# Taking most of the last maximum while the last rows still load, and splitting the early stores

## The chip, the cores and the metric

The kernel runs on one core of a Trainium2 chip. The metric is device time in microseconds (us) of one execution.

In the profile, DVE is VectorE, ACT is ScalarE, POOL is GpSimd and SP is SyncE, which in the kernels before and after issues the loads. A name with a q (SPq, POOLq) is that engine's sequencer. L48 is line 48 of the kernel. The *span* is what the profile covers, from the first instruction to the last; it is 1.8 to 1.9 us shorter than the time. Each run lists the span of every execution, rounded to 0.1 us. The trace of each profiled execution has the span to 0.001 us (320.545 before); stretches that run to the end of the span are taken from it.

## The reference

```python
B, N, D = 8, 4096, 512
gram = np.matmul(x, y.transpose(0, 2, 1))
diag = np.diagonal(gram, axis1=1, axis2=2)
diag = diag - diag.max(axis=-1, keepdims=True)
exp = np.exp(diag)
return exp / exp.sum(axis=-1, keepdims=True)
```

Only the diagonal is needed: 4096 dot products of length 512 in each of 8 batches, then a softmax over the 4096 numbers of a batch. The work on the data takes less time than reading it: 134 MB have to be read.

## The kernel before

A batch lies on 128 partitions with R = 32 rows each, so its dot products are a tile of 128 x 32: "column r" holds the dot products of row r of every partition. The first five batches share one softmax (group a), the next two share another (group b), and the last batch has its own. Only this last one cannot hide behind loads. To keep it short, the last batch is loaded in ever smaller pieces, down to one row.

```python
def dot_row(b, r):                      # one column of 128 dot products
    nc.vector.scalar_tensor_tensor(out=xt[:, r, :], in0=xt[:, r, :], scalar=1.0,
        in1=ys[:, r, :], op0=Alu.mult, op1=Alu.mult, accum_out=diag[:, b, r : r + 1])

def group_out(name, b0, n, ssum):       # scale and store a group
    # ... (reciprocal and scaling cut)
    nc.scalar.dma_start(out=ov[:, b0 : b0 + n, :], in_=res[:, b0 : b0 + n, :])

def last_softmax(b):
    db, rb = diag[:, b, :], res[:, b, :]
    # ... (columns cut)
    nc.vector.tensor_reduce(out=mxp, in_=db, axis=X, op=Alu.max)
    nc.gpsimd.partition_all_reduce(out_ap=mx, in_ap=mxp, channels=P, reduce_op=bass_isa.ReduceOp.max)
    nc.vector.tensor_single_scalar(out=nmx, in_=mx, scalar=-1.0, op=Alu.mult)
    nc.scalar.activation(out=rb, in_=db, func=Act.Exp, bias=nmx, scale=1.0, accum_out=sump)
    nc.gpsimd.partition_all_reduce(out_ap=ssum, in_ap=sump, channels=P, reduce_op=bass_isa.ReduceOp.add)
    nc.vector.reciprocal(out=rc, in_=ssum)
    nc.vector.tensor_single_scalar(out=rb, in_=rb, scalar=rc, op=Alu.mult)
    nc.scalar.dma_start(out=ov[:, b, :], in_=rb)

# ... (batches 0 to 6 cut)
b = B - 1
r0 = 0
for n in (8, 8, 8, 4, 2, 1, 1):
    load_x(b, r0, n)                    # both on the SyncE queue
    load_y(b, r0, n)
    for r in range(r0, r0 + n):
        if r == 2:
            second = group_exp("b", B - 3, 2)
        if r == 10:
            group_out("b", B - 3, 2, second)
        dot_row(b, r)
    r0 += n
last_softmax(b)
```

In this program every DMA signals its completion on one of eight semaphores, in turn (DMA 0 on the first, DMA 8 on the first again); the trace numbers them S99 to S101 and S103 to S107. In the traces, a DMA that is to use a semaphore is issued only when the DMA that used it before has landed. So adding one store shifts which earlier DMA each later load waits for.

Of the kernel before, what the change touches and what calls it, by code (L numbers as in the profile page):

```python
# [1 line left out]

# [5 lines left out]


@with_exitstack
def kernel(
    ctx: ExitStack,
    tc: tile.TileContext,
    x: bass.AP,
    y: bass.AP,
    out: bass.AP,
):
    nc = tc.nc
    ctx.enter_context(tc.manual_schedule())  # L20
    f32 = mybir.dt.float32
    Alu = mybir.AluOpType
    Act = mybir.ActivationFunctionType
    X = mybir.AxisListType.X
    B, N, D = x.shape
    P = nc.NUM_PARTITIONS
    R = N // P
    wide = B - 2


    xv = x.rearrange("b (p r) d -> b p r d", p=P)
    yv = y.rearrange("b (p r) d -> b p r d", p=P)
    ov = out.rearrange("b (p r) -> p b r", p=P)

    big = ctx.enter_context(tc.tile_pool(name="big", bufs=1))
    small = ctx.enter_context(tc.tile_pool(name="small", bufs=1))


    xs = [big.tile([P, R, D], f32, name=f"xs{i}") for i in range(2)]
    ys = big.tile([P, R, D], f32, name="ys")  # L40
    diag = small.tile([P, B, R], f32, name="diag")
    res = small.tile([P, B, R], f32, name="res")

    def column(name, n):
        return small.tile([P, n], f32, name=name)

    def load_x(b, r0, n):
        nc.sync.dma_start(out=xs[b % 2][:, r0 : r0 + n, :], in_=xv[b, :, r0 : r0 + n, :])  # L48

    def load_y(b, r0, n):  # L50
        nc.sync.dma_start(out=ys[:, r0 : r0 + n, :], in_=yv[b, :, r0 : r0 + n, :])

    def dots_wide(b, r0, n):
        xt = xs[b % 2][:, r0 : r0 + n, :]
        nc.vector.tensor_tensor(out=xt, in0=xt, in1=ys[:, r0 : r0 + n, :], op=Alu.mult)  # L55

    def sums_wide(b):
        nc.vector.tensor_reduce(out=diag[:, b, :], in_=xs[b % 2], axis=X, op=Alu.add)  # L58

    def dot_row(b, r):  # L60
        xt = xs[b % 2]
        nc.vector.scalar_tensor_tensor(  # L62
            out=xt[:, r, :],
            in0=xt[:, r, :],
            scalar=1.0,
            in1=ys[:, r, :],
            op0=Alu.mult,
            op1=Alu.mult,
            accum_out=diag[:, b, r : r + 1],
        )  # L70

    def group_exp(name, b0, n):

        mxp, mx, nmx, sump, ssum = (column(name + s, n) for s in ("mxp", "mx", "nmx", "sump", "ssum"))
        nc.vector.tensor_reduce(out=mxp, in_=diag[:, b0 : b0 + n, :], axis=X, op=Alu.max)  # L75
        nc.gpsimd.partition_all_reduce(out_ap=mx, in_ap=mxp, channels=P, reduce_op=bass_isa.ReduceOp.max)  # L76
        nc.scalar.mul(nmx, mx, -1.0)  # L77
        for i in range(n):
            nc.scalar.activation(  # L79
                out=res[:, b0 + i, :], in_=diag[:, b0 + i, :], func=Act.Exp,  # L80
                bias=nmx[:, i : i + 1], scale=1.0, accum_out=sump[:, i : i + 1],
            )
        nc.gpsimd.partition_all_reduce(out_ap=ssum, in_ap=sump, channels=P, reduce_op=bass_isa.ReduceOp.add)  # L83
        return ssum

    def group_out(name, b0, n, ssum):
        rc = column(name + "rc", n)
        nc.vector.reciprocal(out=rc, in_=ssum)  # L88
        for i in range(n):
            rb = res[:, b0 + i, :]  # L90
            nc.scalar.activation(out=rb, in_=rb, func=Act.Copy, scale=rc[:, i : i + 1])  # L91
        nc.scalar.dma_start(out=ov[:, b0 : b0 + n, :], in_=res[:, b0 : b0 + n, :])

    def last_softmax(b):
        db, rb = diag[:, b, :], res[:, b, :]
        mxp, mx, nmx, sump, ssum, rc = (column("l" + s, 1) for s in ("mxp", "mx", "nmx", "sump", "ssum", "rc"))
        nc.vector.tensor_reduce(out=mxp, in_=db, axis=X, op=Alu.max)  # L97
        nc.gpsimd.partition_all_reduce(out_ap=mx, in_ap=mxp, channels=P, reduce_op=bass_isa.ReduceOp.max)  # L98
        nc.vector.tensor_single_scalar(out=nmx, in_=mx, scalar=-1.0, op=Alu.mult)  # L99
        nc.scalar.activation(out=rb, in_=db, func=Act.Exp, bias=nmx, scale=1.0, accum_out=sump)  # L100
        nc.gpsimd.partition_all_reduce(out_ap=ssum, in_ap=sump, channels=P, reduce_op=bass_isa.ReduceOp.add)  # L101
        nc.vector.reciprocal(out=rc, in_=ssum)  # L102
        nc.vector.tensor_single_scalar(out=rb, in_=rb, scalar=rc, op=Alu.mult)  # L103
        nc.scalar.dma_start(out=ov[:, b, :], in_=rb)

    for b in range(wide):
        load_x(b, 0, R)
        for r0 in (0, R // 2):
            load_y(b, r0, R // 2)
            dots_wide(b, r0, R // 2)  # L110
        if b == wide - 1:
            group_out("a", 0, wide - 1, first)
        sums_wide(b)
        if b == wide - 2:
            first = group_exp("a", 0, wide - 1)

    b = B - 2
    load_x(b, 0, R)
    for r0 in (0, R // 2):
        load_y(b, r0, R // 2)  # L120
        for r in range(r0, r0 + R // 2):
# [5 lines that stand above are left out]
        load_x(b, r0, n)  # L127
        load_y(b, r0, n)
        for r in range(r0, r0 + n):
            if r == 2:  # L130
                second = group_exp("b", B - 3, 2)
            if r == 10:
                group_out("b", B - 3, 2, second)
            dot_row(b, r)
        r0 += n
    last_softmax(b)


# [1 line left out]
_INS = ['x', 'y']  # L140
_OUTS = [((8, 4096), 'float32')]


# [23 lines left out]
```

## Time and profile before

| | before |
|---|---|
| time, median of the first runs | 322.76 us (322.57 to 322.77) |
| span of the profiled execution | 320.5 us |
| last row of y landed | 314.97 us |
| start of the last row's product to end of span | 5.48 us |
| last store issued to end of span | 2.41 us |

First, lines of the page of the kernel before: the span, the busy time of VectorE, the two DMA queues (packets, MB, share of 16 engines' span; q1 carries the loads and q10 the stores), and the lines of the chain of work that ended last.

```profile
span 320.5 us, 318 instructions
...
DVE 248.9 (78%) x154; ACT 6.2 (2%) x26; POOL 3.3 (1%) x10
...
q1 hardware_dynamic: 5040, 134.22, 97.4%
q10 hardware_dynamic: 1072, 0.13, 0.3%
...
DMA ys<-in_y_dram 74%; DVE xs L55 16%; DVE xs L62 4%; DMA out_dram<-res 3%; SPq L48 0%; POOLq L162 0%; ACT res L91 0%; POOL lmx L98 0%; DVE res L103 0%; DVE lmxp L97 0%; DVE lrc L102 0%; DVEq L55 0%; DVE brc L88 0%; DVEq L62 0%; DVEq L103 0
```

The load queue is busy for 97.4% of the span and VectorE for 78%. The loads bound this kernel, and the table of windows shows until when. Its columns are the window, its length and DVE's busy time, then those of ACT and POOL, the clock, the DMA share and GB/s:

```profile
300.00:305.00 5.00, 0.22 (x3) 0.00 (x0) 0.00 (x0) 1.00 0.98 412
...
310.00:313.00 3.00, 3.00 (x11) 0.00 (x0) 0.00 (x0) 1.00 1.03 391
313.00:314.00 1.00, 0.89 (x5) 0.00 (x0) 0.00 (x0) 1.00 0.72 262
314.00:315.00 1.00, 0.50 (x2) 0.00 (x0) 0.00 (x0) 1.00 0.03 12
```

The DMA engines are full until 313 us and nearly idle from 314 us. What counts after that is the timeline of the tail (start, duration, engine, line, operation; in brackets the idle time before it and what ended it):

```profile
313.80 0.69 DVE L62 SCALAR_TENSOR_TENSOR xs<-xs,ys 128x512 f32<-128x512 f32 x1
314.42 0.08 DVE L62 DVE_READ_ACCUMULATOR xs<-xs,ys 128x1 f32 x1
315.06 0.69 DVE L62 SCALAR_TENSOR_TENSOR xs<-xs,ys 128x512 f32<-128x512 f32 x1 [0.56 <-DMA ys<-in_y_dram]
315.68 0.08 DVE L62 DVE_READ_ACCUMULATOR xs<-xs,ys 128x1 f32 x1
315.80 0.19 DVE L97 TENSOR_REDUCE lmxp<-diag 128x1 f32<-128x32 f32 x1
316.07 0.37 POOL L98 PARTITION_ALL_REDUCE lmx<-lmxp  x1 [26.66 <-DVE lmxp L97]
316.48 0.15 DVE L99 TENSOR_SCALAR lnmx<-lmx 128x1 f32<-128x1 f32 x1 [0.49 <-POOL lmx L98]
316.66 0.32 ACT L100 ACTIVATE res<-diag,lnmx 128x32 f32<-128x32 f32 x1 [19.62 <-DVE lnmx L99]
...
317.17 0.40 POOL L101 PARTITION_ALL_REDUCE lssum<-lsump  x1 [0.72 <-ACT res L100]
...
318.14 0.35 ACTq L104 DMA_DIRECT2D out_dram<-res  x1
```

Row 31's product starts at 315.06, 0.09 us after its y landed, and its accumulator is read until 315.76. Then the 32-column maximum runs (315.80), the maximum over partitions (316.07), the negation (316.48), the exponential (316.66), the sum over partitions (317.17), and the store is issued at 318.14. Each waits for the one before.

The load queue's own waits, from 270 us on, hold one wait of a load for a store (total, times, longest):

```profile
SPq L48 <- DMA out_dram<-res: 7.4, 1, 7.4
```

This is the x load of row 31. By the rotation of the semaphores it waits for the store of group b, issued at 297.07 and landed 10.5 us later, at 307.58; the load was issued at 307.60. The chain puts this store on the path that ended last.

### The profile page before, as it was taken

How to read it: one execution, taken by the hardware profiler on the slowest of the kernel's cores; microseconds unless marked ns; L12 is line 12 of the kernel's file. 1: busy time of each engine (PE TensorE's matmuls, PEld its weight loads, DVE VectorE, ACT ScalarE, POOL GpSimd, SP SyncE). 2: the span in 40 equal slices, each digit the busy share in tenths (PEclk: the TensorE clock that was granted, in tenths of full speed). 3: DMA queues.
4: the chain of work that ended last, by engine and by line, in shares of the span. 5: the costliest groups of instructions: out<-in, count | busy, mean ns of one | idle time of the engine just before them, and what ended most of it. 6: DMA issues, size and time to landing. Idle time of an engine off the chain costs nothing.

```text
span 320.5 us, 318 instructions
## 1 busy us (share of the span) xinstructions
DVE 248.9 (78%) x154; ACT 6.2 (2%) x26; POOL 3.3 (1%) x10
## 2 busy tenths in 40 slices
DVE  0000989969999689996899968998789969994494
ACT  1000000000000000000000000000101000010000
POOL 0000000000000000000000000000000000000000
DMA  9999999899999999989999999999999999999991
GB/s 393 393 393 458 429 421 523 348 438 491 425 393 429 421 458 401 515 364 421 515 401 393 442 409 458 450 401 450 401 523 393 394 448 407 425 429 427 421 410 59
DMA packets 6113, 134.36 MB, mean 419 GB/s; under 512 B 1632, under 2 KB 1632, under 8 KB 2400
## 3 DMA queue, kind: packets, MB, share of 16 engines
q1 hardware_dynamic: 5040, 134.22, 97.4%
q10 hardware_dynamic: 1072, 0.13, 0.3%
q14 instruction: 1, 0.01, 0.0%
HBM read 134.22 MB, written 0.13 MB: 419 GB/s over the span
## 4 chain that ended last, share of the span: by engine, by line
DMA 77%; DVE 20%; issue 1%; SPq 0%; POOLq 0%; ACT 0%; POOL 0%; DVEq 0%; ACTq 0%
DMA ys<-in_y_dram 74%; DVE xs L55 16%; DVE xs L62 4%; DMA out_dram<-res 3%; SPq L48 0%; POOLq L162 0%; ACT res L91 0%; POOL lmx L98 0%; DVE res L103 0%; DVE lmxp L97 0%; DVE lrc L102 0%; DVEq L55 0%; DVE brc L88 0%; DVEq L62 0%; DVEq L103 0%
## 5 line engine op out<-in xcount | busy, mean ns | idle before, releaser
L55 DVE TENSOR_TENSOR xs<-xs,ys 128x8192 f32<-128x8192 f32 x12 | 104.3, 8692 | 53.6 <-DMA ys<-in_y_dram 53.6
L58 DVE TENSOR_REDUCE diag<-xs 128x32 f32<-128x16384 f32 x6 | 103.3, 17220 | 0.2
L62 DVE SCALAR_TENSOR_TENSOR xs<-xs,ys 128x512 f32<-128x512 f32 x64 | 40.0, 688 | 13.8 <-DMA ys<-in_y_dram 13.6
L62 DVE DVE_READ_ACCUMULATOR xs<-xs,ys 128x1 f32 x64 | 5.3, 83 | 0.0
L77 ACT ACTIVATE anmx<-amx 128x5 f32<-128x5 f32 x1 | 0.2, 208 | 221.9 <-POOL amx L76 221.9
L76 POOL PARTITION_ALL_REDUCE amx<-amxp x1 | 0.4, 386 | 223.1 <-DVE amxp L75 223.1
L79 ACT ACTIVATE res<-diag,anmx 128x32 f32<-128x32 f32 x5 | 1.5, 309 | 0.0
L91 ACT ACTIVATE res<-res,arc 128x32 f32<-128x32 f32 x5 | 1.2, 309 | 19.0 <-DVE arc L88 19.0
L76 POOL PARTITION_ALL_REDUCE bmx<-bmxp x1 | 0.7, 736 | 60.5 <-DVE bmxp L75 60.5
L77 ACT ACT_TABLE_LOAD x1 | 1.3, 1283 | 0.7 <-PEq L151 0.7
L77 ACT ACTIVATE bnmx<-bmx 128x2 f32<-128x2 f32 x1 | 0.2, 203 | 41.6 <-POOL bmx L76 41.6
L79 ACT ACTIVATION_READ_ACCUMULATOR res<-diag,anmx 128x1 f32 x5 | 0.9, 187 | 0.0
L102 DVE RECIPROCAL lrc<-lssum 128x1 f32<-128x1 f32 x1 | 0.2, 162 | 1.0 <-POOL lssum L101 1.0
L83 POOL PARTITION_ALL_REDUCE bssum<-bsump x1 | 0.8, 797 | 1.1 <-ACT res L79 1.1
L100 ACT ACTIVATE res<-diag,lnmx 128x32 f32<-128x32 f32 x1 | 0.3, 321 | 19.6 <-DVE lnmx L99 19.6
L91 ACT ACTIVATE res<-res,brc 128x32 f32<-128x32 f32 x2 | 0.5, 313 | 8.0 <-DVE brc L88 8.0
L98 POOL PARTITION_ALL_REDUCE lmx<-lmxp x1 | 0.4, 367 | 26.7 <-DVE lmxp L97 26.7
L79 ACT ACTIVATE res<-diag,bnmx 128x32 f32<-128x32 f32 x2 | 0.6, 314 | 0.0
L99 DVE TENSOR_SCALAR lnmx<-lmx 128x1 f32<-128x1 f32 x1 | 0.2, 153 | 0.5 <-POOL lmx L98 0.5
L83 POOL PARTITION_ALL_REDUCE assum<-asump x1 | 0.5, 459 | 2.0 <-ACT res L79 2.0
L101 POOL PARTITION_ALL_REDUCE lssum<-lsump x1 | 0.4, 397 | 0.7 <-ACT res L100 0.7
L79 ACT ACTIVATION_READ_ACCUMULATOR res<-diag,bnmx 128x1 f32 x2 | 0.4, 188 | 0.0
(11 smaller groups left out, 1.9 us busy)
## 6 DMA issues: line engine op xcount, KB each, us to landing
ys<-in_y_dram SPq DMA_DIRECT2D x14, 4096.0 KB, 30.0
xs<-in_x_dram SPq DMA_DIRECT2D x3, 2048.0 KB, 19.5
ys<-in_y_dram SPq DMA_DIRECT2D x3, 2048.0 KB, 19.9
xs<-in_x_dram SPq DMA_DIRECT2D x1, 1024.0 KB, 26.6
ys<-in_y_dram SPq DMA_DIRECT2D x1, 1024.0 KB, 27.0
xs<-in_x_dram SPq DMA_DIRECT2D x1, 512.0 KB, 25.9
ys<-in_y_dram SPq DMA_DIRECT2D x1, 512.0 KB, 22.2
xs<-in_x_dram SPq DMA_DIRECT2D x2, 256.0 KB, 12.4
```

What stands on the lines that cost most here:

```text
L55: nc.vector.tensor_tensor(out=xt, in0=xt, in1=ys[:, r0 : r0 + n, :], op=Alu.mult)
L58: nc.vector.tensor_reduce(out=diag[:, b, :], in_=xs[b % 2], axis=X, op=Alu.add)
L62: nc.vector.scalar_tensor_tensor(out=xt[:, r, :], in0=xt[:, r, :], scalar=1.0, in1=ys[:, r, :], op0=Alu.mult, op1=Alu.mult, accum_out=diag ...
L76: nc.gpsimd.partition_all_reduce(out_ap=mx, in_ap=mxp, channels=P, reduce_op=bass_isa.ReduceOp.max)
L77: nc.scalar.mul(nmx, mx, -1.0)
L79: nc.scalar.activation(out=res[:, b0 + i, :], in_=diag[:, b0 + i, :], func=Act.Exp, bias=nmx[:, i : i + 1], scale=1.0, accum_out=sump[:, i ...
L83: nc.gpsimd.partition_all_reduce(out_ap=ssum, in_ap=sump, channels=P, reduce_op=bass_isa.ReduceOp.add)
L91: nc.scalar.activation(out=rb, in_=rb, func=Act.Copy, scale=rc[:, i : i + 1])
L98: nc.gpsimd.partition_all_reduce(out_ap=mx, in_ap=mxp, channels=P, reduce_op=bass_isa.ReduceOp.max)
L99: nc.vector.tensor_single_scalar(out=nmx, in_=mx, scalar=-1.0, op=Alu.mult)
L100: nc.scalar.activation(out=rb, in_=db, func=Act.Exp, bias=nmx, scale=1.0, accum_out=sump)
L101: nc.gpsimd.partition_all_reduce(out_ap=ssum, in_ap=sump, channels=P, reduce_op=bass_isa.ReduceOp.add)
```

## The change

Its intent is to shorten the tail. The maximum of columns 0 to 29 is taken between rows 29 and 30 and written as a 33rd column beside the data. The maximum over partitions then takes three columns (30, 31 and that one) as soon as row 31 is done, and the negation becomes a negated maximum of three. The early stores become four DMAs instead of two, five with the last.

```diff
-    diag = small.tile([P, B, R], f32, name="diag")
+    diag = small.tile([P, B - 1, R], f32, name="diag")
+    last = small.tile([P, R + 1], f32, name="last")
...
-            accum_out=diag[:, b, r : r + 1],
+            accum_out=last[:, r : r + 1] if b == B - 1 else diag[:, b, r : r + 1],
...
-        nc.scalar.dma_start(out=ov[:, b0 : b0 + n, :], in_=res[:, b0 : b0 + n, :])
+        for i, j in ((b0, b0 + n - 1), (b0 + n - 1, b0 + n)):
+            nc.scalar.dma_start(out=ov[:, i:j, :], in_=res[:, i:j, :])
...
-        nc.vector.tensor_reduce(out=mxp, in_=db, axis=X, op=Alu.max)
-        nc.gpsimd.partition_all_reduce(out_ap=mx, in_ap=mxp, channels=P, reduce_op=bass_isa.ReduceOp.max)
-        nc.vector.tensor_single_scalar(out=nmx, in_=mx, scalar=-1.0, op=Alu.mult)
...
+        nc.gpsimd.partition_all_reduce(
+            out_ap=mx, in_ap=last[:, R - 2 :], channels=P, reduce_op=bass_isa.ReduceOp.max
+        )
+        nc.vector.tensor_reduce(out=nmx, in_=mx, axis=X, op=Alu.max, negate=True)
...
+            if r == R - 2:
+                nc.vector.tensor_reduce(out=last[:, R:], in_=last[:, : R - 2], axis=X, op=Alu.max)
```

More of the change, by code (lines that the diff above doesn't have):

```diff
@@ L91, in group_out @@
             nc.scalar.activation(out=rb, in_=rb, func=Act.Copy, scale=rc[:, i : i + 1])
-        nc.scalar.dma_start(out=ov[:, b0 : b0 + n, :], in_=res[:, b0 : b0 + n, :])
+        for i, j in ((b0, b0 + n - 1), (b0 + n - 1, b0 + n)):
+            nc.scalar.dma_start(out=ov[:, i:j, :], in_=res[:, i:j, :])
     def last_softmax(b):
-        db, rb = diag[:, b, :], res[:, b, :]
-        mxp, mx, nmx, sump, ssum, rc = (column("l" + s, 1) for s in ("mxp", "mx", "nmx", "sump", "ssum", "rc"))
-        nc.vector.tensor_reduce(out=mxp, in_=db, axis=X, op=Alu.max)
-        nc.gpsimd.partition_all_reduce(out_ap=mx, in_ap=mxp, channels=P, reduce_op=bass_isa.ReduceOp.max)
-        nc.vector.tensor_single_scalar(out=nmx, in_=mx, scalar=-1.0, op=Alu.mult)
+        db, rb = last[:, :R], res[:, b, :]
+        mx = column("lmx", 3)
+        nmx, sump, ssum, rc = (column("l" + s, 1) for s in ("nmx", "sump", "ssum", "rc"))
+        nc.gpsimd.partition_all_reduce(
+            out_ap=mx, in_ap=last[:, R - 2 :], channels=P, reduce_op=bass_isa.ReduceOp.max
+        )
+        nc.vector.tensor_reduce(out=nmx, in_=mx, axis=X, op=Alu.max, negate=True)
         nc.scalar.activation(out=rb, in_=db, func=Act.Exp, bias=nmx, scale=1.0, accum_out=sump)
```

## The prediction

> **What bounds the kernel.** The loads. The page shows 134.22 MB read in a span of 320.5 us, the load queue busy for 97.4% of 16 engines' span; VectorE is busy for 78%. In the table of windows the DMA share is about 1.0 until 313 us and 0.03 after 314 us. The chain of waits is 74% loads of y. Only what follows the landing of the last row is exposed. By the timeline: last y row landed 314.97; row product 315.06 to 315.76; maximum of 32 columns 315.80 to 315.99; GpSimd maximum 316.07 to 316.44; negation to 316.63; exp from 316.66; GpSimd sum 317.17 to 317.57; store issued at 318.14. So the tail is about 5.5 us (314.97 to 320.5), 1.7% of the span.
>
> **The change, costed.**
> 1. The 32-column maximum leaves the tail. It costs 315.76 to 315.99 there: 0.23 us. GpSimd now follows the last row product directly, about 0.08 us after it (its gap now).
> 2. The GpSimd maximum takes 3 columns instead of 1. That with 5 columns (stage "a") took 0.386 us, with 1 column 0.367: +0.01.
> 3. The negation (0.153) becomes a negated maximum of 3 columns, about 0.16: +0.01.
> 4. The 30-column maximum, about 0.2 us, goes between rows 29 and 30, where VectorE is idle from 313.68 to 313.80 waiting for row 30. Row 30 starts about 0.1 to 0.15 us later and ends by 314.65, before row 31 lands (314.97). Cost 0.
> 5. Stores: 5 instead of 3, same bytes and packets. Two more issues on ScalarE (0.38 us each) are off the chain. But DMAs take completion semaphores in turn, eight of them, so loads now wait for other predecessors. Before, the x load of row 31 waited for store "b" (307.60; in the chain). After, by the instruction order: x of rows 16 to 23 waits for the 4-column store "a" (issued 246; I estimate landing at 280 to 283, from 640 packets in 40.4 us), issue 275.4 -> about 281; y of row 30 waits for the first part of "b" (about 304 instead of 299.9); x of row 31 for the second part (about 307.6 to 308, unchanged); others move up to 5 us. All stay ahead of the queue: at 281 us loads landing until 295 are outstanding, and rows 30 and 31 start moving only at about 311 to 312. Stores are slow because their packets take turns with the loads': the Trainium skill, "DMA: Bandwidth & Descriptors", section "Queues, rings and completion order", says that each engine round-robins between queues by packet; this trace agrees (40 packets per engine, 40.4 us). Cost 0.
>
> **On the chain:** 0.23 - 0.02, about 0.2 us, 0.07%. Predicted 322.55 us, range 322.2 to 322.95. Faster by over 2%: 0.005; within 2%: 0.98; slower: 0.015.
>
> **What would show it.** Last row landing at 315 +- 0.3 us in the new trace; last product's end to GpSimd start about 0.1 us instead of 0.31; GpSimd maximum 0.36 to 0.40; negated maximum under 0.2; landing to end of span about 5.3 us; waits of the load queue on stores at row 16's x and row 30's y too, with the DMA share still 1.0 until 313.
>
> **What would make it wrong.** The load queue running dry because a load waits for a split store (a dip of the DMA share after 290 us): +1 to 5 us. The 30-column maximum holding up row 31. Scatter of the last landing may hide 0.2 us.

## The result, and the profile after

| | before | after |
|---|---|---|
| time, median (range), 4 runs each | 322.69 us (322.57 to 322.77) | 322.58 us (322.11 to 322.86) |
| ratio, 95% interval | | 0.9996 (0.9978 to 1.0013) |
| span of the profiled execution | 320.5 us | 320.9 us |
| last row of y landed | 314.97 us | 315.71 us |
| start of the last row's product to end of span | 5.48 us | 5.13 us |
| last store issued to end of span | 2.41 us | 2.26 us |

Ratios here and below are the mean time of one kernel's runs over that of the other's of the same rounds, so not quite the ratio of the medians quoted. The predicted 322.55 us is met within 0.03 us. But the interval of the ratio spans 0.35%, or 1.1 us, so the time alone proves nothing about a gain of 0.2 us. The profiled execution of the changed kernel was even the slowest of its four, 0.4 us longer in span than the profiled one of before.

The same lines of the page of the changed kernel:

```profile
span 320.9 us, 323 instructions
...
DVE 248.8 (78%) x154; ACT 6.2 (2%) x26; POOL 3.3 (1%) x10
...
q1 hardware_dynamic: 5040, 134.22, 97.4%
q10 hardware_dynamic: 1104, 0.13, 0.3%
...
DMA ys<-in_y_dram 74%; DVE xs L57 16%; DVE xs L64 4%; DMA out_dram<-res 3%; SPq L50 0%; POOLq L169 0%; ACT res L93 0%; POOL lmx L101 0%; DVE res L108 0%; DVE lrc L107 0%; ACTq L95 0%; DVEq L57 0%; DVE brc L90 0%; DVEq L64 0%; DVEq L108 0%
```

Hardly anything moved there but the number of packets on the store queue, 1104 instead of 1072. The same windows show full DMA engines until 313 us again:

```profile
300.00:305.00 5.00, 0.86 (x4) 0.00 (x0) 0.00 (x0) 1.00 0.97 408
...
310.00:313.00 3.00, 3.00 (x11) 0.00 (x0) 0.00 (x0) 1.00 1.03 394
313.00:314.00 1.00, 0.90 (x5) 0.00 (x0) 0.00 (x0) 1.00 0.78 285
314.00:315.00 1.00, 0.96 (x4) 0.00 (x0) 0.00 (x0) 1.00 0.07 27
```

The tail of the changed kernel in the timeline:

```profile
314.59 0.18 DVE L138 TENSOR_REDUCE last<-last 128x1 f32<-128x30 f32 x1
314.69 0.68 DVE L64 SCALAR_TENSOR_TENSOR xs<-xs,ys 128x512 f32<-128x512 f32 x1
315.30 0.08 DVE L64 DVE_READ_ACCUMULATOR xs<-xs,ys 128x1 f32 x1
315.80 0.69 DVE L64 SCALAR_TENSOR_TENSOR xs<-xs,ys 128x512 f32<-128x512 f32 x1 [0.42 <-DMA ys<-in_y_dram]
316.42 0.08 DVE L64 DVE_READ_ACCUMULATOR xs<-xs,ys 128x1 f32 x1
316.60 0.37 POOL L101 PARTITION_ALL_REDUCE lmx<-last  x1 [26.42 <-DVE xs L64]
317.00 0.16 DVE L104 TENSOR_REDUCE lnmx<-lmx 128x1 f32<-128x3 f32 x1 [0.50 <-POOL lmx L101]
317.19 0.32 ACT L105 ACTIVATE res<-last,lnmx 128x32 f32<-128x32 f32 x1 [19.36 <-DVE lnmx L104]
...
317.70 0.40 POOL L106 PARTITION_ALL_REDUCE lssum<-lsump  x1 [0.73 <-ACT res L105]
...
318.68 0.34 ACTq L109 DMA_DIRECT2D out_dram<-res  x1
```

From the end of row 31's accumulator read (316.50) to the GpSimd maximum (316.60) there is 0.10 us, where 0.31 us passed before (315.76 to 316.07). Counted from the start of row 31's product, which takes out when the row landed, the exponential comes after 1.39 us instead of 1.60. The 30-column maximum (314.59) sits ahead of row 30, and VectorE still idles for 0.42 us before row 31, so it cost nothing. The GpSimd maximum took 0.37 us with three columns as with one, and the negated maximum 0.16.

The load queue's waits for stores, from 270 us on:

```profile
SPq L50 <- DMA out_dram<-res: 8.6, 2, 6.5
...
SPq L53 <- DMA out_dram<-res: 4.9, 1, 4.9
```

There are three of them now: 6.5 us at the x load of rows 16 to 23 (issued at 282.24 instead of 275.40), 4.9 us at the y load of row 30 (305.92 instead of 299.90), and 2.1 us at the x load of row 31 (308.39 instead of 307.60).

Two things were open. The last row landed 0.74 us later in this profile: chance, or the price of the new waits? And the stretch after the last store got shorter by 0.15 us, which the prediction had not foreseen.

### The profile page after: what moved, and what is told of

Its sections match the earlier page's. It is cut to its first block, busy times and chain, and to the rows that moved or that the text cites. A ratio compares the mean times of both kernels' runs of the same rounds, so it can differ in the third digit from the quotient of the medians. Undisturbed runs are those within 1.5% of the kernel's fastest.

```text
span 320.9 us, 323 instructions
## 1 busy us (share of the span) xinstructions
DVE 248.8 (78%) x154; ACT 6.2 (2%) x26; POOL 3.3 (1%) x10
## 3 DMA queue, kind: packets, MB, share of 16 engines
q10 hardware_dynamic: 1104, 0.13, 0.3%
## 4 chain that ended last, share of the span: by engine, by line
DMA 78%; DVE 20%; issue 1%; SPq 0%; POOLq 0%; ACT 0%; POOL 0%; DVEq 0%; ACTq 0%
DMA ys<-in_y_dram 74%; DVE xs L57 16%; DVE xs L64 4%; DMA out_dram<-res 3%; SPq L50 0%; POOLq L169 0%; ACT res L93 0%; POOL lmx L101 0%; DVE res L108 0%; DVE lrc L107 0%; ACTq L95 0%; DVEq L57 0%; DVE brc L90 0%; DVEq L64 0%; DVEq L108 0%
```

## The experiments

My theory was that the tail is about 0.2 us shorter, that the stores cost nothing because the load queue stays full, and that the landing of the last row scatters from execution to execution. The main rival was that the split stores delay the loads and eat a gain of 0.4 us or more. Twelve kernels ran, each timed in five rounds, four to a chip, and all gave correct results. The kernel before took a mean of 322.57, 322.57 and 322.53 us on the three chips (9 runs each), so chips need no correction here.

| run | mean us | ratio (95% interval) | mean span us | product start to end of span | last store issued to end of span |
|---|---|---|---|---|---|
| before, beside e1 to e4 | 322.57 | | 320.78 | 5.48 (first profile) | 2.41 |
| e1 the kernel before, unchanged | 322.59 | 1.0001 (0.9988 to 1.0014) | 320.78 | 5.49 | 2.41 |
| e2 maximum only | 322.54 | 1.0000 (0.9987 to 1.0012) | 320.74 | 5.28 | 2.41 |
| e3 stores only | 322.54 | 1.0000 (0.9986 to 1.0013) | 320.62 | 5.34 | 2.26 |
| e4 whole change | 322.40 | 0.9995 (0.9983 to 1.0008) | 320.48 | 5.13 | 2.26 |
| e5 heavy store | 324.83 | 1.0070 (1.0057 to 1.0083) | 322.90 | 5.12 | 2.26 |
| e6 group b's stores late | 322.00 | 0.9982 (0.9969 to 0.9995) | 320.20 | 5.12 | 2.26 |
| e7 twelve maxima | 324.67 | 1.0068 (1.0055 to 1.0082) | 322.30 | 5.12 | 2.26 |
| e8 early shift | 321.88 | 0.9978 (0.9966 to 0.9991) | 319.96 | 4.53 | 2.25 |
| e9 all early stores late, four DMAs | 322.12 | 0.9990 (0.9976 to 1.0003) | 320.34 | 5.17 | 2.30 |
| e10 the same in one DMA | 322.54 | 1.0001 (0.9989 to 1.0014) | 320.64 | 5.37 | 2.51 |
| e11 e8 and e9 together | 321.50 | 0.9969 (0.9956 to 0.9981) | 319.72 | 4.56 | 2.29 |
| e12 whole change, beside e9 to e11 | 322.38 | 0.9996 (0.9983 to 1.0009) | 320.46 | 5.12 | 2.25 |

The last two columns come from each run's single profile. "Product start" is the start of row 31's product. Mean span less this tail is an estimate of when the product starts on average, and so of the mean landing of the last row, good to about 0.1 us: 315.27 to 315.32 in the kernel before on the three chips, 315.28 in e3, 315.46 in e2, 315.35 and 315.34 in e4 and e12 (315.47 in the four executions of the first comparison), 315.08 in e6, 315.17 in e9.

### e1: the kernel before once more

No edit.

> The kernel before, unchanged, to see the scatter. Every theory: ratio 1.000 within 0.001 of the kernel before. The theory (scatter of the last landing): single times spread over 0.3 to 0.8 us; the last row of this profile lands anywhere from 314.6 to 315.8; from that landing to the end of the span 5.5 us as before (within 0.05).

It came as expected for ratio and tail. The five times spread over 0.33 us, and row 31's product started at 315.35 instead of 315.06. The tail repeats to 0.01 us while the landing does not. So the tail is to be read from one profile, and the landing only from many executions.

### e2: the maximum alone

```diff
-        for i, j in ((b0, b0 + n - 1), (b0 + n - 1, b0 + n)):
-            nc.scalar.dma_start(out=ov[:, i:j, :], in_=res[:, i:j, :])
+        nc.scalar.dma_start(out=ov[:, b0 : b0 + n, :], in_=res[:, b0 : b0 + n, :])
```

(against the changed kernel)

> Only the maximum is moved; stores stay 3. Theory (the tail is shorter by about 0.2 us, the store change costs nothing): mean 0.2 us under the kernel before (ratio 0.9993, hard to tell from 1), landing to end of span 5.2 us instead of 5.5, gap from the last product to the GpSimd maximum about 0.1. Rival (the split stores delay the loads, which ate a gain): this run is clearly better than the whole change, by 0.4 us or more, and its last row lands by 315.0.

The tail is 5.28 us, 0.21 shorter than before, and the exponential starts 1.39 us after the product instead of 1.60. The time moved by 0.03 us only, which five runs cannot tell from 0.2: by the estimate above the product started 0.17 us later in these executions than in the kernel before (315.46 against 315.29). It is not better than the whole change (322.54 against 322.40 in e4), where the rival asked for 0.4 us or more, so the rival fails here.

### e3: the stores alone

```diff
-        nc.scalar.dma_start(out=ov[:, b0 : b0 + n, :], in_=res[:, b0 : b0 + n, :])
+        for i, j in ((b0, b0 + n - 1), (b0 + n - 1, b0 + n)):
+            nc.scalar.dma_start(out=ov[:, i:j, :], in_=res[:, i:j, :])
```

(against the kernel before)

> Only the stores are split; the 32-column maximum stays in the tail. Theory: time as the kernel before within 0.2 us, landing to end of span 5.5 us, although the load queue waits for stores at the x load of row 16 (issue near 282 us) and at the y load of row 30 (near 306). Rival: slower than the kernel before by 0.4 us or more, last landing at 315.5 or later.

The time is that of the kernel before within 0.03 us, row 30's y was issued at 305.37, and row 31's product started at 315.27, earlier than in the twin. The rival's delay of 0.4 us is not there, though the interval of the ratio reaches it (1.0013 is 0.42 us): the estimated mean start of the product, 315.28, is that of the kernel before, 315.29. The tail should have stayed as it was, but it is 5.34 us instead of 5.48, and all of the difference lies after the last store was issued (2.26 us instead of 2.41).

### e4 and e12: the whole change again

No edit to the changed kernel.

> The whole change once more, beside the parts. Theory: as the tail alone within 0.2 us, about 0.2 under the kernel before; landing to end of span 5.2 us. Rival: slower than the tail alone by 0.4 us or more.

> The changed kernel on the same chip as these, to compare with: 0.1 to 0.4 us under the kernel before, ratio 0.9995; start of the last row's product to end of span 5.1 us.

Both gave a tail of 5.12 to 5.13 us, a mean span of 0.30 us under the kernel before on the same chip (320.48 against 320.78, 320.46 against 320.76) and a mean time of 0.17 and 0.15 us under it. Row 31's product started at 315.07 and 315.20 (in the fastest and the second fastest of five executions), and its estimated mean start is 0.06 to 0.07 us later than in the kernel before, which is within its error. So the late landing of the first profile, 0.74 us, was chance.

### e5: a store that lands too late

The first store of group b also rewrites batches 0 to 4 with the values they already have.

```diff
-        for i, j in ((b0, b0 + n - 1), (b0 + n - 1, b0 + n)):
+        for i, j in ((0, b0 + n - 1), (b0 + n - 1, b0 + n)):
```

> The changed kernel with the first part of the second store made six batches wide (it writes batches 0 to 4 again, with the same values), so that it lands late and holds the y load of row 30 that waits for its completion semaphore. Theory (loads do wait for stores, but there is a slack of some 6 us between the issue of row 30's y and the moment the queue needs it): the slack is used up, y of row 30 is issued at 312 us or later, the load queue runs dry and the DMA share dips before the end, kernel slower by 1 to 2.5 us. Rival (such waits don't matter at all, the queue holds enough in any case): within 0.3 us of the kernel before. Rival (split stores already cost time): slower too, so not told apart here.

It is 2.26 us slower than the kernel before. The windows of this run:

```profile
310.00:312.00 2.00, 2.00 (x9) 0.00 (x0) 0.00 (x0) 1.00 1.01 374
312.00:314.00 2.00, 1.84 (x7) 0.00 (x0) 0.00 (x0) 1.00 0.08 21
314.00:315.00 1.00, 0.35 (x3) 0.00 (x0) 0.00 (x0) 1.00 0.61 156
```

And from its timeline, the y load of row 30 and what VectorE does next (the two products are rows 30 and 31):

```profile
313.23 0.33 SPq L53 DMA_DIRECT2D ys<-in_y_dram  x1
...
314.20 0.18 DVE L138 TENSOR_REDUCE last<-last 128x1 f32<-128x30 f32 x1
316.16 0.69 DVE L64 SCALAR_TENSOR_TENSOR xs<-xs,ys 128x512 f32<-128x512 f32 x1 [1.78 <-DMA ys<-in_y_dram]
...
317.68 0.69 DVE L64 SCALAR_TENSOR_TENSOR xs<-xs,ys 128x512 f32<-128x512 f32 x1 [0.82 <-DMA ys<-in_y_dram]
```

The y load of row 30 was held until 313.23. By then the queue had been empty for a us: the DMA share is 0.08 from 312 to 314 us. VectorE idles 1.78 us before row 30. So loads do wait for stores, and such a wait costs time as soon as it outlasts the queue. The heavy store also adds 40 small packets on each DMA engine, but row 29's y, loaded before the hold, landed at 312.76, between 312.35 (e4) and 313.15 (the first profile), so no cost of theirs is seen. In the changed kernel the same load was issued at 305 to 306 us, some 5 us before the DMA engines started on the one-row loads (their first packets run at about 310.7 us in the trace).

### e6: no late load waits for a store of group b

```diff
-            if r == 10:
+            if r == R - 1:
                 group_out("b", B - 3, 2, second)
```

> The changed kernel with the second group's scaling and stores put after the loads of the last row, so that no load of rows 28 to 31 waits for them and their packets don't interleave with the loads. Theory: nothing to gain, the load queue was always full: within 0.2 us of the changed kernel; landing to end of span 5.2 us. Rival (the waits of row 30 and 31 on stores delay the last landing): faster than the changed kernel by 0.4 us or more, last landing earlier than 315.0.

It missed the expectation, on the rival's side: the mean is 0.57 us under the kernel before on its chip, against 0.15 to 0.17 for the changed kernel on others, and the span 0.60 against 0.30. The profile does not show it well, since the profiled execution was the slowest of the five and its last landing no earlier (product at 315.27). Of the 0.4 us by which it leads the changed kernel of the other chips, 0.12 us lie outside the span (1.80 against 1.92 us) and about 0.27 us in an earlier start of the product (315.08 against 315.34 and 315.35). I then had two explanations: the waits themselves, or the time that the store's packets take on the DMA engines. The kernel before, whose store "b" is one DMA, has no earlier start (315.27 to 315.32), so what e6 gained is not a price of the split.

### e7: twelve maxima

```diff
-                nc.vector.tensor_reduce(out=last[:, R:], in_=last[:, : R - 2], axis=X, op=Alu.max)
+                for _ in range(12):
+                    nc.vector.tensor_reduce(out=last[:, R:], in_=last[:, : R - 2], axis=X, op=Alu.max)
```

> The changed kernel with the 30-column maximum taken twelve times in its place between rows 29 and 30. Theory (one costs nothing since VectorE waits about 0.4 us before row 31): eleven more at 0.12 to 0.19 us are 1.3 to 2.1 us, of which about 0.4 us is hidden, so slower than the changed kernel by 0.9 to 1.7 us, with no wait left before row 31. Rival (one already delayed the end): slower by the full 1.3 to 2.1 us, and no idle time before row 31 in the changed kernel either.

The timeline around them:

```profile
313.69 2.59 DVE L139 TENSOR_REDUCE last<-last 128x1 f32<-128x30 f32 x12
316.19 0.68 DVE L64 SCALAR_TENSOR_TENSOR xs<-xs,ys 128x512 f32<-128x512 f32 x1
...
316.80 0.69 DVE L64 SCALAR_TENSOR_TENSOR xs<-xs,ys 128x512 f32<-128x512 f32 x1
```

Twelve took 2.5 us (313.69 to 316.19), 0.22 us each rather than the 0.12 to 0.19 that I had assumed, and pushed row 30 back by eleven of them, 2.4 us. The span grew by 1.83 us over that of the changed kernel (322.30 against 320.47, the mean of e4 and e12). So about 0.6 us was hidden and the idle time before row 31 is real: a single maximum fits into it. The profile alone says the same: row 31's y landed at 314.87 and its product started at 316.80, 1.84 us later than the usual 0.09 us after landing. The time missed the expectation (0.9 to 1.7 us): it grew by 2.28 us, which taken alone would speak for the rival, as eleven maxima cost 2.4. But 0.45 us of it lie outside the span, where VectorE's wait for row 31 cannot be: 2.37 us on average here, 1.92 in the changed kernel.

### e8: the shift from the first 30 columns only

Any shift gives the same softmax as long as nothing overflows. Here it is the maximum of the first 30 columns, so nothing of it waits for the last two rows.

```diff
...
-        nc.gpsimd.partition_all_reduce(
-            out_ap=mx, in_ap=last[:, R - 2 :], channels=P, reduce_op=bass_isa.ReduceOp.max
-        )
-        nc.vector.tensor_reduce(out=nmx, in_=mx, axis=X, op=Alu.max, negate=True)
...
             if r == R - 2:
                 nc.vector.tensor_reduce(out=last[:, R:], in_=last[:, : R - 2], axis=X, op=Alu.max)
+                lmx, lnmx = column("lmx", 1), column("lnmx", 1)
+                nc.gpsimd.partition_all_reduce(
+                    out_ap=lmx, in_ap=last[:, R:], channels=P, reduce_op=bass_isa.ReduceOp.max
+                )
+                nc.scalar.mul(lnmx, lmx, -1.0)
...
```

> The shift of the exponent is taken from the first 30 columns alone (the softmax is the same for any shift; these inputs do not overflow): the maximum over partitions and the negation run while the last rows load, and nothing of the maximum is left in the tail. Theory (only what follows the last landing counts): the GpSimd maximum 0.37, the negation 0.16 and two hand-overs, about 0.6 us in all, leave the tail: 0.6 us faster than the changed kernel, 0.8 than the kernel before (ratio 0.9975); landing to end of span 4.6 us. Rival (the time is set by scatter of the loads and the tail is not worth counting): no difference in the time beyond 0.2 us.

The timeline shows the maximum and the negation ahead of row 31's product, and the exponential right after it:

```profile
314.60 0.73 POOL L135 PARTITION_ALL_REDUCE lmx<-last  x1 [24.70 <-DVE last L133]
...
315.36 0.20 ACT L138 ACTIVATE lnmx<-lmx 128x1 f32<-128x1 f32 x1 [17.79 <-POOL lmx L135]
315.59 0.69 DVE L64 SCALAR_TENSOR_TENSOR xs<-xs,ys 128x512 f32<-128x512 f32 x1 [0.48 <-DMA ys<-in_y_dram]
316.21 0.08 DVE L64 DVE_READ_ACCUMULATOR xs<-xs,ys 128x1 f32 x1
316.39 0.32 ACT L100 ACTIVATE res<-last,lnmx 128x32 f32<-128x32 f32 x1 [0.82 <-DVE xs L64]
```

The tail is 4.53 us and the span 0.84 us under the kernel before, as expected; the time is 0.69 us under it. The kernel is faster (the interval excludes 1). A shorter tail does shorten the time, once it is large enough to be seen over the scatter.

### e9 and e10: all early stores after the loads

The four early stores are issued by SyncE behind the load of row 31 (e9), or one store of all seven batches is (e10).

```diff
-        for i, j in ((b0, b0 + n - 1), (b0 + n - 1, b0 + n)):
-            nc.scalar.dma_start(out=ov[:, i:j, :], in_=res[:, i:j, :])
...
+            if r == R - 1:
+                for i, j in ((0, 4), (4, 5), (5, 6), (6, 7)):    # e10: ((0, 7),)
+                    nc.sync.dma_start(out=ov[:, i:j, :], in_=res[:, i:j, :])
             dot_row(b, r)
```

> The changed kernel, but the stores of groups a and b (same scaling, 4 DMAs) are issued by the load queue's engine after the load of the last row, so that none of their 56 packets per DMA engine runs between loads. The last store stays on the last of the eight semaphores in the order of the closing waits. Theory P (each small packet takes about 14 ns of its engine: 0.3% of the span for about 1,070 packets; 16 of them after the loads explain half of the last run's gain): 56 x 14 ns = 0.8 us of load time are freed, about 0.7 us faster than the changed kernel, ratio to the kernel before about 0.997. Theory W (what was gained came from waits of rows 30 and 31 on stores): no better than the run with only group b late, ratio about 0.998. Chance: within 0.2 us of the changed kernel. Last store's issue to end of span 2.25 us.

> As the run with four, but one store for all seven batches, so that the last store falls on the fifth of the eight semaphores. Theory (at the end the load queue's engine goes through the semaphores in a fixed order at 0.063 us each, and the last store was third from the end before the change and is last after it): three more waits follow the last store's landing, so 2.43 us from its issue to the end of the span instead of 2.25. Rival (the 0.12 us that the split saved at the end come from fewer bytes or packets still in flight): 2.25 us here too, or less.

e9 gained 0.26 us on the changed kernel of the same chip (322.12 against 322.38). That is far from the 0.7 us of theory P, and moving 56 packets per DMA engine gained no more than moving 16 in e6. P is refuted in the size that I gave it. W named a ratio of about 0.998; 0.9990 was measured, with an interval that holds 0.998 and 1. And more than half of the 0.26 us, 0.14, lies outside the span (1.78 us against 1.92), where no instruction of the profile runs; the spans differ by 0.12 us only, which is within their scatter. Whether moving the stores behind the loads gains anything besides is seen in e6 alone, and by what stays open.

e10 settles the other question. The instructions with which SyncE ends the program, from the trace (start in us; S103 to S107 are five of the eight completion semaphores, S107 the last that is looked at):

```
before  319.602 wait S105 (last store)   319.666 wait S106   319.728 wait S107   319.793 drain
after                                                        320.119 wait S107 (last store)   320.184 drain
e10     319.459 wait S104 (last store)   319.526 wait S105   319.590 wait S106   319.652 wait S107   319.717 drain
```

SyncE goes through the semaphores in a fixed order, 0.06 to 0.07 us each. Where the last store signals on S105, two waits that are long satisfied still follow; after the change it signals on S107 and none does. In e10 it signals on S104, three follow, and the stretch is 2.51 us instead of 2.30 (0.19 us in the three waits and 0.02 to 0.03 in the landing). This is what the split of the stores buys: of the 0.15 us of e3, 0.13 is the place of the last store in the rotation; the other 0.02 us, a slightly earlier landing of that store (1.42 us after its issue instead of 1.45), is not explained.

### e11: e8 and e9 together

> Early shift and late stores on the load queue together. If both gains are independent: 0.6 us under the run with four late stores, 1.3 under the changed kernel; 321.1 us or less, ratio to the kernel before about 0.995. From the start of the last row's product to the end of the span 4.5 us.

It is e9 with the edit of e8. The median is 321.39 us, 1.1 us under the kernel before and less than hoped, but the gains nearly add up: by the means 0.69 (e8) and 0.41 (e9), together 1.03. It beats both kernels. It is right for these inputs; an input whose last two rows exceed all others of a batch by so much that the exponential overflows would break it, so it is not a replacement as it stands.

## Why the prediction was right

**The bound (right).** DMA engines full until 313 us and only the tail exposed: the windows after say the same.

**Steps 1 to 3, the maximum (right, shown).** Predicted were 0.23 us out and 0.02 us back in. The gap to the GpSimd maximum went from 0.31 to 0.10 us, that maximum took 0.37 us and the negated one 0.16, and the exponential comes 0.21 us earlier in every profile of the moved maximum (e2, e4, e12).

**Step 4, the 30-column maximum costs nothing (right, shown for VectorE).** VectorE still waits 0.42 to 0.57 us before row 31 in the profiles with it, and in e7 some 0.6 us of added work was hidden. That the moved maximum makes the last row land later by some 0.1 us is not excluded: the estimated starts of e2, e4 and e12 lie 0.06 to 0.17 us above those of the kernel before.

**Step 5, the stores cost nothing (right for the time; incomplete).** The three waits came about where predicted: the x load of rows 16 to 23 at 282.2 us (about 281 predicted), row 30's y at 305.9 (about 304), row 31's x at 308.4 (307.6 to 308). e3 shows no cost in time beyond the scatter, and e5 shows that there is a limit and that it was some us away. The round robin between queues that the prediction quotes from the Trainium skill, "DMA: Bandwidth & Descriptors", section "Queues, rings and completion order", agrees again: the second part of store "a" still needs 40.5 us to land, as the whole of it did (40.4). Between the first and the last of the 640 packets of store "a" in the kernel before, the trace has 583 load packets, nearly one for one. What the prediction missed is that the split also shortens the end of the span, by 0.15 us in e3, nearly all of it through the order of the closing waits.

**The sum.** The tail became 0.35 us shorter (5.48 to 5.13), 0.21 from the maximum and about 0.15 after the last store, mostly from the closing waits, and the mean span fell by 0.30. Yet the time fell by 0.15 to 0.17. The rest lies in the difference between time and span, which was 1.77 to 1.81 us on average in the kernel before (on three chips, and as e1) and in e2, but 1.92 in e3, e4 and e12. So the 0.15 us that the split won inside the span was about given back outside it, and the means of e4 and e12 come near the predicted 0.2 us. The prediction of 322.55 was met partly because two terms that it lacked cancel; that it was met within 0.03 us is luck, as the four executions ran from 322.11 to 322.86. Why the time outside the span differs between these kernels was not found; it does not follow the number of stores alone, since e10 with two has 1.90 and e9 with five 1.78. In the traces it goes with the number of SyncE's instructions: 71 or 78 in every kernel with 1.77 to 1.81 us (before, e1, e2, e6, e9, e11), 72 in every kernel with 1.90 to 1.93 (after, e3, e4, e5, e8, e10, e12) and in e7. No run varied that number alone, so this is no cause shown.

**"Scatter of the last landing may hide 0.2 us" (right).** It did: in the first comparison the last row landed at 315.71, outside the 315 +- 0.3 us that the prediction had named as a sign (314.98 and 315.11 in e4 and e12), the profiled execution after was longer than the one before, and no interval of the ratio excludes 1 for the whole change. What stands for the gain is the tail in the profiles and the equal shift of the mean span on two chips, not the verdict of the clock.

## What to carry to other kernels

In a kernel bound by loads, read a small change in the tail from the moment the last data lands, in the profile, where it repeats to about 0.01 us (5.12 to 5.13 in six profiles with this tail); end-to-end times scatter by more than such a change is worth. Before moving or splitting DMAs, list which load will wait for which earlier DMA and compare the delay with how far ahead the queue is: a wait in the chain, even one that "ended last", cost nothing here while the queue behind it was full, and 2.26 us once it ran dry (e5). Where a maximum is only a shift for safety, ask whether it has to wait for the last data at all.

## What the Trainium skill lacked or had wrong

- "DMA: Bandwidth & Descriptors", section "Why a DMA increments its semaphore by 16 and not by 1", asks for one semaphore per in-flight slot. It does not say what follows when eight are used in turn: a load waits for whatever used its semaphore before, a slow small store included. Here that was 7.4 us of waiting at one load before the change and 13.5 us at three loads after it (without a cost that e3 shows), and 2.26 us of the kernel's time in e5.
- No page that I read has the cost of the closing waits: 0.06 to 0.07 us for each semaphore looked at after that of the last store (0.13 us for the two that the split saved, 0.19 for the three in e10).
- "Runtime: NRT & Kernel Launch", section "The ~15µs preamble/postamble breakdown", is about another gap: there a profile's total is longer than the reported execution time, by about 6.2 us in every kernel (6.02 to 6.67). Here the time is longer than the span, by 1.78 us on average in e9, 1.92 in e4 and e12, 2.37 in e7 (eleven more instructions than e12). No page that I read has this gap or says what sets it.
- "SBUF — State Buffer", section "Who interferes with whom", says that a VectorE instruction with two SBUF inputs contends with a GpSimd instruction that reads SBUF. The traces fit that: the maximum over partitions took 0.73 us in e8 and e11 while a product of two SBUF tiles ran, and 0.37 us in the tail with VectorE idle. The page gives no time for this pair; here it is about a factor of two, and no run varied the overlap alone.
